# Narrower weights in one of the two products with V: 68 of 128 columns, and V kept as high, low in every head

## The chip, the cores and the metric

The kernel runs on one core of a Trainium2 chip. The metric is the device time of one execution in microseconds (us). The kernel before was timed three times: 2116.72, 2116.77 and 2116.83 us, median 2116.77 us. One further execution was recorded by the hardware profiler; its page and trace are what the text below reads.

The engines have short names in the profile: PE is the matrix engine, PEld its weight loads (which overlap its products), DVE the vector engine, ACT the scalar engine, POOL the engine for general work, SP the one that starts most transfers. Times are us unless marked ns.

## The reference

The model is a decoder trunk of two layers over 1024 positions with 1024 channels. Layer 0 mixes tokens by a gated unit in chunks of 128 positions, layer 1 by a dilated attention; each is followed by a feed-forward block with squared ReLU. The part that matters here is the attention, cut to its core:

```python
def _dilated_group(q, k, v, bias_table, window, dilation):
    ...
    s = jnp.einsum('bnqrhc,bnkrhc->bnrhqk', qb, kc) * (HEAD_DIM ** -0.5)
    ...
    m = jnp.max(logits, axis=-1)
    p = jnp.exp(logits - m[..., None])
    den = jnp.sum(p, axis=-1)
    num = jnp.einsum('bnrhqk,bnkrhc->bnqrhc', p, vc)
```

There are 8 heads of 64 channels and three groups with (window, dilation) = (128, 1), (512, 4) and (2048, 16). Their numerators and denominators are merged for each head, and the quotient goes through an output projection. The last line, the numerator, is the product that the change touches.

## The kernel before

All large products are made with numbers split in two: a high half, rounded to the matrix engine's format, and a low half, what the rounding left. A product of two split numbers is then the sum of high by high, high by low and low by high. Helpers record every such operation: line 197 issues each matrix product, line 204 each transposition through the matrix engine, lines 225 and 226 the two halves of a split (ACT rounds, DVE subtracts).

The attention is worked off in twelve units: four pairs of heads, and for each the three groups. For a unit the queries and keys are computed by seven products of blocks (`unit_qk`, written out in program order). Beside them run three generators for every unit's four steps: `scores` (queries by keys, then bias, minimum and exponential on DVE and ACT), `turned` (the probabilities transposed by the matrix engine and split into a high half `ph` and a low half `pl`), and `values` (the product with V). The order on the matrix engine is fixed while the program is written: a clock that counts each product by the columns of its moving operand (`flow.pe`) says when a generator's next step is due. The count does not look at how many columns the weights have.

V is computed once for all positions before the attention. `value_store` splits it and writes it to DRAM, 64 columns of a half at a time: tile `vs` has shape (128 positions, 4 pairs of heads, 4 quarters, 64). Before the change the quarters of a pair of heads A, B are: A high, A low, B low, B high. `v_load` fetches a pair's 256 columns back into two tiles `V`.

In `values` the two heads of a pair are handled one after the other. For each block of 128 keys the weights are two quarters of V, that is 128 columns with one head's high and low half; they are loaded twice, once for the product with `ph` (e = 0) and once for the product with `pl` (e = 1). A product's moving operand is 128 or 256 columns wide (one or two blocks of queries). All of them add up in one bank `pv`: 64 of its rows hold the sum with V's high half, the other 64 the sum with V's low half. Lines 1551 and 1552 then add the two sets of rows: ACT copies one into `N`, DVE adds the other. Of the four products of halves, low by low is included before the change.

There are 432 products with V in all: for a pair of heads 32 with dilation 4, 32 with dilation 16 and 44 with dilation 1. In the profile they are `at<-tr,V`, and `at<-p,V` in the last unit. Half of them are of the kind e = 1.

Of the kernel before, what the change touches and what calls it, by code (L numbers as in the profile page):

```python
# [19 lines left out]
P = 128  # L20
# [15 lines left out]
def blk(b, n=1):  # L36
    return slice(b * P, (b + n) * P)
# [81 lines left out]
STEPS = (5, 3)  # L119
ROOTS = ((0, 7, 0, 1, 0), (1, 7, 0, 1, 2))  # L120
GATE, ROWS, RB = 6, 10000, 5
ASIDE = {768: (4,)}
EARLY = 4
PACE = (1700.0, 1800.0, 3000.0)
# [4 lines left out]
def trunk(ctx: ExitStack, tc: tile.TileContext, xT, w_u, w_v, w_o, w_s, b_s, w_qkv, w_vt, w_bo, rel,  # L129
# [23 lines left out]
    def slot(shape=(P, S), dtype=F32, name="s"):  # L153

        return slots.tile(list(shape), dtype, tag="s", name=name)
# [37 lines left out]
    def at_bank():  # L193
        return psa.tile([P, HALF], F32, tag="at", name="at")

    def matmul(out, lhsT, rhs, passes=1, **kw):
        nc.tensor.matmul(out, lhsT, rhs, **kw)  # L197
        n = 1
        for d in rhs.shape[1:]:
            n *= d  # L200
        flow.pe(max(n, 64) * COL * passes)
# [26 lines left out]
    def weight(src, own=None):  # L228
        lo = wpool.tile([P, D], F32R, tag="w", name="wlo")
        hi = wpool.tile([P, D], F32R, tag="w", name="whi")  # L230
        for i in range(2):
            split(hi[:, half(i)], lo[:, half(i)], load(src[:, half(i)], own and own()))
        return hi, lo
# [500 lines left out]
    for gi, chunks in enumerate(((0, 1, 2), (3, 4, 5), (6, 7))):  # L734
        banks = {}
        for k in range(KT):
# [7 lines left out]
            with tc.issue_after(roots[0] if k == 1 else gelus[5]) if gi == 1 and k else nullcontext():  # L744
                w = weight(w_v[k])
# [26 lines left out]
            for e, i, n, f in order:  # L772
                x, c = ys[n // 4][k], blk(n % 4)
                matmul(banks[n, f], x[e == 1][:, c], w[e == 2][:, half(f)], start=(k == 0 and e == 0),
                       stop=(k == 7 and e == 2))
# [29 lines left out]
    for tiles in ((0, 1, 2), (3,), (4,), (5, 6, 7)):  # L805
        w = [weight(w_u[m]) for m in tiles]
# [14 lines left out]
    for tiles in ((0, 1), (2,), (3,), (4, 5, 6, 7)):  # L821
        w = [weight(w_o[m]) for m in tiles]
# [359 lines left out]
    hd = [[dram.tile([P, HALF], F32, name=f"hd{m}_{s}", bufs=1) for s in range(2)] for m in range(KT)]  # L1182
# [51 lines left out]
    for hp, g in units:  # L1234
        u = Unit()
# [52 lines left out]
    def value_store(r, b, src):  # L1288
        v = slot((P, 4, 4, 64), F32R, "vs")
        p4 = src.rearrange("p (u a c) -> p u a c", u=4, a=2)  # L1290
        hi, lo = v[:, :, 0:4:3, :], v[:, :, 1:3, :]
        nc.scalar.activation(hi, p4, AF.Copy)
        nc.vector.tensor_tensor(lo, p4, hi.bitcast(F32), op=ALU.subtract)
        nc.sync.dma_start(vd[r][blk(b)], v.bitcast(F32))
# [24 lines left out]
    def all_values():  # L1319

        operands, wv = value_operands(), []
        for s in range(2):
            ks = range(KT) if s == 0 else [4 * j + k for k in range(4) for j in range(2)]
            banks = [mm_bank() if s == 0 and x < 3 else at_bank() for x in range(4)]
            for n, k in enumerate(ks):
                y = terms_a.blocks[k // 4, s]
                flow.until(lambda: len(y) > k % 4)
                for b, bank in enumerate(banks):
                    x, w, c = y[k % 4], firsts[k], blk(b)
                    matmul(bank, x.hi[:, c], w.hi, start=(k == 0), stop=False)  # L1330
                    matmul(bank, x.hi[:, c], w.lo, start=False, stop=False)
                    matmul(bank, x.lo[:, c], w.hi, start=False, stop=(k == KT - 1))
                    flow.pump()
                if s:
                    wv.append(next(operands))
            for b, bank in enumerate(banks):
                value_store(0, 4 * s + b, bank)
# [10 lines left out]
        for n, p in enumerate(VSEQ):  # L1348
# [11 lines left out]
            for b, bank in enumerate(banks):  # L1360
                u, k1 = uk[b][:, 0, :], uk[b][:, 1, :]
                for k in range(4):
                    flow.until(lambda: len(x) > k)
                    c, last = blk(b), k == 3
                    matmul(bank, x[k].hi[:, c], w[k].hi, start=k == 0 and opens, stop=False, skip_group_check=True)
                    matmul(bank, x[k].hi[:, c], w[k].lo, start=False, stop=False, skip_group_check=True)
                    matmul(bank, x[k].lo[:, c], w[k].hi, start=False, stop=last, skip_group_check=True)
                    flow.pump()
                if p in (1, 6):
                    nc.scalar.activation(u, bank, AF.Copy)  # L1370
                elif p == 2:
                    value_store(1, b, added(u, bank))
                elif p == 5:
                    nc.scalar.activation(k1, bank, AF.Copy)
                elif p == 7:
                    value_store(2, 4 + b, added(k1, bank))
                elif p == 3:
                    value_store(1, 4 + b, added(u, bank))
                else:
                    value_store(2, b, bank)  # L1380
                if 0 < n < 6:
                    wv.append(next(operands))
                elif n == 6 and b:
                    more()
# [26 lines left out]
    def place(g, kb):  # L1411

        return (kb % 2, kb // 2) if g == 1 else (kb // 4, kb % 4)
# [66 lines left out]
    def geometry(g, j):  # L1480

        if g == 2:
            keys = [(2 * j, 1), (2 * j + 1, 1)]
        elif g == 1:
            keys = [(2 * j, 1), (2 * j, 2)]
        else:
            keys = [(2 * j - 1, 2) if j else (0, 1), (2 * j, 2)]
        at = [0, keys[0][1] * P]
        return keys, at, at[1] + keys[1][1] * P
# [40 lines left out]
    def values(u, j, pts):  # L1530
        keys, at, _ = geometry(u.g, j)

        parts = {}
        for i in range(2):
            for x in range(keys[i][1]):
                parts.setdefault(keys[i][0] + x, []).append((at[i] + x * P, i * P))
        pv = at_bank()
        for hd in range(2):
            lst = list(parts.items())
            for n, (kb, cs) in enumerate(lst):  # L1540
                pc, oc, w = cs[0][0], hd * 2 * P + cs[0][1], len(cs) * P
                tv, at_ = place(u.g, kb)
                va = u.V[tv][:, at_, 2 * hd:2 * hd + 2, :]
                for e in range(2):
                    matmul(pv[:, oc:oc + w], va, pts[hd][e][:, pc:pc + w], start=(hd == 0 and n == 0 and e == 0),
                           stop=(n == len(lst) - 1 and e == 1), skip_group_check=True)
        for hd in range(2):
            r, x = slice(64 * hd, 64 * hd + 64), slice(64 - 64 * hd, 128 - 64 * hd)
            o, c = u.N[r, 2 * j * P:(2 * j + 2) * P], slice(hd * 2 * P, (hd + 1) * 2 * P)
            with tc.high_priority(offset=PRIO):  # L1550
                nc.scalar.activation(o, pv[x, c], AF.Copy)
                nc.vector.tensor_tensor(o, o, pv[r, c], op=ALU.add)
# [41 lines left out]
    def valuer():  # L1594
        for n, (i, j) in enumerate(seq):
            u = U[i]
            yield turned_at[n], LAT["turn"]
            yield u.v, 0
            if j == 0:
                if u.hp > 0:  # L1600
                    yield rested[u.hp - 1], 0
                u.N = slot(name="N")
            yield from turn_for(CALM[2])
            values(u, j, turned_p.pop(n))
            valued_at[n].t = flow.t
            if j == 3:
                u.pv.t = flow.t
            if u.g == 0 and j % 2:
                valued[u.hp, j // 2].t = flow.t
            yield 0  # L1610
# [242 lines left out]
    def final(sq):  # L1853
# [5 lines left out]
        out = outT.rearrange("(k p) t -> p k t", p=P)  # L1859
        aside = ASIDE.get(sq.cols.start, ())  # L1860
        if aside:
# [89 lines left out]
```

## Time and profile before

| what | value |
|---|---|
| timed, median of three | 2116.77 us |
| the profiled execution, first to last instruction | 2116.2 us |
| granted clock of the matrix engine, mean | 0.998 |
| PE busy | 2093.6 us (99%), 10160 products |
| PEld busy | 1731.2 us (82%), 10160 loads |
| DVE busy, ACT busy | 1577.5 us (75%), 1182.7 us (56%) |
| products with V | from 1085.1 to 1443.7 us of the span |

Some 0.5 us of the timed median lies outside the profiled span. In a row of the profile, `at<-tr,V 128*128 128x256` means: written is a bank `at`, read are the moving operand `tr` and the weights `V`, the array is used with 128 rows by 128 columns, and the moving operand has 256 columns. Products and loads are pipelined: the recorded length of one is longer than the step from one to the next, so a rate is read from several in a row.

### The profile page before, as it was taken

What the parts mean: (1) busy time and instruction counts of PE and PEld (TensorE: products, weight loads), DVE (VectorE), ACT (ScalarE), POOL (GpSimd) and SP (SyncE); (2) the same over time, 40 slices, a digit from 0 to 9 for tenths busy, and PEclk for the clock granted to TensorE, in tenths of its full rate; (3) what the DMA queues carried; (4) which work ended last, traced back from release to release, by engine and by line L of the source; (5) the groups of instructions that cost most, each with busy time, mean ns of one, the idle gap of its engine ahead of it and who ended that gap; (6) DMA issues with size and microseconds to landing.
All of it is one profiled execution on the core that took longest, in us unless ns stands there. A gap on an engine that the chain in (4) does not pass through costs nothing.

```text
span 2116.2 us, 30735 instructions
## 1 busy us (share of the span) xinstructions
PE 2093.6 (99%) x10160; PEld 1731.2 (82%) x10160; DVE 1577.5 (75%) x2902; ACT 1182.7 (56%) x2387; POOL 495.5 (23%) x368
## 2 busy tenths in 40 slices
PE   9999999999999999999999999999999999999998
PEld 7888888888888888788888888888888888888887
DVE  7878769766689999787746666757985456988876
ACT  7645436566675555345456665776556556544432
POOL 2000124323224333430000000002442222433244
PEclk9999999999999999999999999999999999999999
DMA  6428814588766666644865657582266443655432
GB/s 220 130 94 294 305 34 139 196 281 278 258 208 204 231 209 225 222 162 164 308 194 160 176 156 185 157 270 79 71 205 198 156 154 127 203 164 161 143 115 80
DMA packets 224757, 387.10 MB, mean 183 GB/s; under 512 B 39898, under 2 KB 67669, under 8 KB 224597
## 3 DMA queue, kind: packets, MB, share of 16 engines
q1 hardware_dynamic: 215456, 383.77, 55.1%
q10 hardware_dynamic: 9140, 1.36, 0.4%
q8 instruction: 80, 1.31, 0.3%
q14 instruction: 81, 0.66, 0.1%
HBM read 252.24 MB, written 132.81 MB: 182 GB/s over the span
## 4 chain that ended last, share of the span: by engine, by line
PE 88%; DVE 6%; DMA 3%; issue 1%; ACT 1%; POOL 0%; SPq 0%; DVEq 0%; POOLq 0%; ACTq 0%
PE mm L197 45%; PE at L197 41%; PE at L204 2%; DVE y L226 1%; DMA t<-in_w_qkv 1%; DVE t L226 1%; DMA r<-in_w_v 1%; DMA h<-in_xT 0%; DVE r L443 0%; DVE hx L226 0%; DVE tr L226 0%; DVE wp L226 0%; DMA t<-hid_(1, 0)_6229 0%; DMA r<-in_w_vt 0%; DVE b L448 0%
## 5 line engine op out<-in xcount | busy, mean ns | idle before, releaser
L226 DVE TENSOR_TENSOR wp<-r,wp 128x512 fp32r<-128x512 f32 (+3 forms) x399 | 328.2, 828 | 121.8 <-ACT wp L225 119.2
L225 ACT ACTIVATE wp<-r 128x512 fp32r<-128x512 f32 (+3 forms) x399 | 236.0, 596 | 316.7 <-PE at L197 194.5
L197 PE MATMUL mm<-t,wp 128*128 128x512 f32 x1368 | 345.2, 396 | 0.2 <-DVE t L1001 0.2
L197 PE MATMUL at<-hx,wp 128*128 128x512 f32 x1452 | 341.1, 389 | 1.7 <-DVE h L1079 1.5
L197 PEld LDWEIGHTS at<-hx,wp 128*128 128x128 f32 x1452 | 272.2, 188 | 60.0 <-DVE h L1079 3.2
L197 PEld LDWEIGHTS mm<-t,wp 128*128 128x128 f32 x1368 | 250.7, 188 | 53.0 <-issue 0.7
L283 POOL TENSOR_TENSOR t<-t 128x512 f32<-128x512 f32 (+1 forms) x60 | 76.2, 1271 | 810.3 <-ACT t L278 808.1
L197 PE MATMUL at<-y,wp 128*128 128x512 f32 x1008 | 245.3, 389 | 0.0
L197 PE MATMUL mm<-hx,wp 128*128 128x512 f32 x984 | 234.3, 389 | 0.1
L197 PEld LDWEIGHTS at<-y,wp 128*128 128x128 f32 x1008 | 189.1, 188 | 39.5 <-issue 0.4
L197 PEld LDWEIGHTS mm<-hx,wp 128*128 128x128 f32 x984 | 184.6, 188 | 38.9 <-ACT mm L1102 0.5
L197 PE MATMUL mm<-y,wp 128*128 128x512 f32 x816 | 210.3, 397 | 1.2 <-DVE y L226 0.6
L381 POOL TENSOR_TENSOR t<-r 128x512 f32<-128x512 f32 (+3 forms) x62 | 82.5, 1331 | 477.7 <-DMA r<-in_w_up 121.3
L197 PEld LDWEIGHTS mm<-y,wp 128*128 128x128 f32 x816 | 149.1, 188 | 33.4 <-DVE y L226 1.1
L226 DVE TENSOR_TENSOR hx<-t,hx 128x512 fp32r<-128x512 f32 x192 | 161.5, 845 | 6.5 <-ACT hx L225 6.3
L197 PE MATMUL mm<-y,whi 128*128 128x512 f32 x512 | 158.4, 390 | 1.2 <-DVE t L789 1.2
L197 PE MATMUL at<-t,wp 128*128 128x512 f32 x552 | 130.6, 389 | 0.0
L225 ACT ACTIVATE hx<-t 128x512 fp32r<-128x512 f32 x192 | 118.7, 627 | 20.8 <-DMA t<-hid 12.5
L383 POOL TENSOR_TENSOR r<-r 128x512 f32<-128x512 f32 (+3 forms) x62 | 91.0, 1468 | 167.2 <-DVE wp L226 146.9
L197 PEld LDWEIGHTS at<-t,wp 128*128 128x128 f32 x552 | 103.6, 188 | 21.5
L1079 DVE TENSOR_TENSOR h<-h,at 128x512 f32<-128x512 f32 x144 | 97.6, 678 | 25.6 <-PE at L197 25.1
L197 PEld LDWEIGHTS mm<-y,whi 128*128 128x128 f32 x512 | 95.5, 188 | 21.0 <-issue 1.6
(247 smaller groups left out, 3481.3 us busy)
## 6 DMA issues: line engine op xcount, KB each, us to landing
t<-hid SPq DMA_DIRECT2D x182, 256.0 KB, 4.2
wd<-tr SPq DMA_DIRECT2D x154, 256.0 KB, 3.1
wp<-wd SPq DMA_DIRECT2D x77, 512.0 KB, 4.2
hid<-t SPq DMA_DIRECT2D x140, 256.0 KB, 2.9
r<-in_w_up SPq DMA_DIRECT2D x120, 256.0 KB, 2.9
r<-in_w_dn SPq DMA_DIRECT2D x80, 256.0 KB, 2.6
hid<-b SPq DMA_DIRECT2D x56, 256.0 KB, 2.9
r<-in_w_v SPq DMA_DIRECT2D x48, 256.0 KB, 3.1
```

Of the source, the lines that this page charges most:

```text
L197: nc.tensor.matmul(out, lhsT, rhs, **kw)
L204: nc.tensor.transpose(out, src, ident)
L225: return (nc.scalar.activation(hi, src, AF.Copy).ins, (engine or nc.vector).tensor_tensor(lo, src, hi.bitcast(F32), op=ALU.subtract).ins)
L226: (engine or nc.vector).tensor_tensor(lo, src, hi.bitcast(F32), op=ALU.subtract).ins)
L283: nc.gpsimd.tensor_tensor(self.acc, self.acc, sq, op=ALU.add)
L381: tt(r3, r[0, 0], r[1, 0], op=ALU.subtract)
L383: tt(r[1, 1], r[1, 0], r[0, 0], op=ALU.subtract)
L1079: return engine.tensor_tensor(hs[i, s], hs[i, s], src, op=ALU.add).ins
```

## The change

Two things are changed. V's quarters in a pair of heads become A high, A low, B high, B low, so that each head's weights begin with its high half. And in `values`, the product with `pl` takes the first 68 of the 128 weight columns: the 64 of V's high half and four of its low half. It writes 68 rows of the bank. The product with `ph` keeps all 128. Of low by low, only four columns of 64 are still computed; the other 60 are left out of the sum.

```diff
+NARROW = 68
...
     def value_store(r, b, src):
         v = slot((P, 4, 4, 64), F32R, "vs")
         p4 = src.rearrange("p (u a c) -> p u a c", u=4, a=2)
-        hi, lo = v[:, :, 0:4:3, :], v[:, :, 1:3, :]
+        hi, lo = v[:, :, 0:4:2, :], v[:, :, 1:4:2, :]
         nc.scalar.activation(hi, p4, AF.Copy)
         nc.vector.tensor_tensor(lo, p4, hi.bitcast(F32), op=ALU.subtract)
         nc.sync.dma_start(vd[r][blk(b)], v.bitcast(F32))
...
             for n, (kb, cs) in enumerate(lst):
                 pc, oc, w = cs[0][0], hd * 2 * P + cs[0][1], len(cs) * P
                 tv, at_ = place(u.g, kb)
-                va = u.V[tv][:, at_, 2 * hd:2 * hd + 2, :]
-                for e in range(2):
-                    matmul(pv[:, oc:oc + w], va, pts[hd][e][:, pc:pc + w], start=(hd == 0 and n == 0 and e == 0),
-                           stop=(n == len(lst) - 1 and e == 1), skip_group_check=True)
+                va = u.V[tv][:, at_, 2 * hd:2 * hd + 2, :].rearrange("p a c -> p (a c)")
+                for e, m in enumerate((P, NARROW)):
+                    matmul(pv[0:m, oc:oc + w], va[:, 0:m], pts[hd][e][:, pc:pc + w],
+                           start=(hd == 0 and n == 0 and e == 0), stop=(n == len(lst) - 1 and e == 1),
+                           skip_group_check=True)
```

No instruction changes its place on any engine, and none is added or removed. On the matrix engine the 216 products with e = 1 have 68 weight columns in place of 128. Here is the end of one group of eight with its neighbours, on PE in the first unit, before (`tr` are the split probabilities, `wp` the weights of queries and keys):

```order
1448 L197 MATMUL at<-tr,V 128x128 x2
1449 L197 MATMUL at<-tr,V 128x256 x2
1450 L197 MATMUL at<-tr,V 128x128 x2
1451 L197 MATMUL mm<-t_9778,wp 128x512 x3
1452 L204 MATMUL at<-ident,t 128x128 x6
```

and the same place with the change:

```order
1449 L198 MATMUL at<-tr,V 128x128
1450 L198 MATMUL at<-tr,V 68x128
1451 L198 MATMUL at<-tr,V 128x256
1452 L198 MATMUL at<-tr,V 68x256
1453 L198 MATMUL at<-tr,V 128x128
1454 L198 MATMUL at<-tr,V 68x128
1455 L198 MATMUL mm<-t_9778,wp 128x512 x3
1456 L205 MATMUL at<-ident,t 128x128 x6
```

A wide and a narrow product now alternate; what stands ahead of them and behind them is the same. Every line number after the new constant is one or more higher.

## The prediction, on record before the changed kernel was run

> **What bounds the kernel now.** I read the page first, from the busy shares to the chain that ended last:
>
> ```profile
> PE 2093.6 (99%) x10160; PEld 1731.2 (82%) x10160; DVE 1577.5 (75%) x2902; ACT 1182.7 (56%) x2387; POOL 495.5 (23%) x368
> ...
> PEclk9999999999999999999999999999999999999999
> ...
> PE 88%; DVE 6%; DMA 3%; issue 1%; ACT 1%; POOL 0%; SPq 0%; DVEq 0%; POOLq 0%; ACTq 0%
> ```
>
> The matrix engine is never long without work, and the chain is 88% its own. The change touches only the stretch with products by V, so I read that stretch (the attention) in the view of busy times, and the chain inside it:
>
> ```profile
> 1085.00:1447.00 362.00, 360.06 (x2295) 298.23 (x2294) 237.11 (x784) 242.73 (x689) 0.00 (x0) 1.00 0.59 176
> ...
> by line: PE mm L197 64.4%; PE at L197 24.0%; PE at L204 10.3%; DVE t L1688 0.8%; DVE tr L226 0.6%; issue 0.0%
> ```
>
> The columns are PE, PEld, DVE, ACT and POOL busy, then the granted clock (1.00), the share of the transfer engines and GB/s. DVE and ACT have a third of the 362 us free, the transfer engines 41%. The chain is the matrix engine's for 98.7%. So here time taken from PE comes off the end, unless PE runs into another engine that it now outruns.
>
> A busy PE can still be limited by its weight loads. The groups of the products with V, each shape by itself:
>
> ```profile
> L197 PEld LDWEIGHTS at<-tr,V 128*128 128x128 f32 x388 | 50.7, 190 | 4.3 <-DVE tr L226 0.9
> L197 PE MATMUL at<-tr,V 128*128 128x128 f32 x276 | 40.3, 260 | 0.0
> L197 PE MATMUL at<-tr,V 128*128 128x256 f32 x112 | 25.3, 304 | 0.0
> L197 PEld LDWEIGHTS at<-p,V 128*128 128x128 f32 x44 | 5.6, 190 | 0.3
> L197 PE MATMUL at<-p,V 128*128 128x128 f32 x28 | 4.4, 255 | 0.0
> L197 PE MATMUL at<-p,V 128*128 128x256 f32 x16 | 3.6, 303 | 0.0
> ```
>
> There are 276 + 28 = 304 products that stream 128 columns and 112 + 16 = 128 that stream 256. Their rate is seen in one group of eight with 128 columns, in the timeline of PEld from the group's second load on, and in the busy times of the V products in the same stretch:
>
> ```profile
> 1120.65 0.86 PEld L197 LDWEIGHTS at<-tr,V 128*128 128x128 f32 x7
> ...
> 1120.64:1121.42 0.78, 0.78 (x8) 0.77 (x7) 1.00 0.24 83
> ```
>
> Seven loads take 0.86 us from the first start to the last end. With 190 ns for the last one, six steps take 0.67 us: **112 ns a step**. PEld is busy for 0.77 of 0.78 us, so it has a load under way all the time. What would the streams need alone? The shortest recorded product with 128 columns has 220 ns, one with 512 columns 389 ns:
>
> ```profile
> L197 PE MATMUL at<-tr,V x388: 220/275/387, 1085.4 to 1430.3; 128*128 128x128 f32 x138, 128*128 128x256 f32 x56
> ...
> L197 PE MATMUL at<-y,wp 128*128 128x512 f32 x1008 | 245.3, 389 | 0.0
> ...
> 1119.28 1.52 PE L197 MATMUL mm<-y,wp 128*128 128x512 f32 x6
> ```
>
> The 384 columns between them cost 169 ns, 0.44 ns each; the last row gives the same rate, (1.52 - 0.389) / 5 = 0.226 us for 512. So 128 columns stream in 56 ns and 256 in 113 ns. Where a product has 128 columns, the next load (112 ns) sets the step, and half of the step the array has nothing to stream. Where it has 256, stream and load are equal.
>
> **The change, part by part.**
>
> *The narrow load.* A load runs under the product ahead of it: that of e = 1 under the product e = 0 of the same block and the same width. So 304 / 2 = 152 narrow loads stand behind a product of 128 columns and 128 / 2 = 64 behind one of 256. The trace has no load of 68 columns. It has six of 8 columns, as a summary of tile `tab` and in the timeline of PEld:
>
> ```profile
> L197 PEld LDWEIGHTS at<-tr,tab x6: 82/84/86, 447.6 to 488.4; 33*8 33x8 f32 x6
> ...
> 447.59 0.09 PEld L197 LDWEIGHTS at<-tr,tab 33*8 33x8 f32 x2 [0.35 <-issue]
> 448.03 0.30 PEld L197 LDWEIGHTS mm<-t,wp 128*128 128x128 f32 x2 [0.35 <-issue]
> ```
>
> A load of 8 columns has 84 ns, one of 128 has 190: 106 ns for 120 columns, 0.88 ns each. The starts agree: two loads of 8 columns take 0.09 us together, so the second began within 0.01 us of the first, where two of 128 in the row below take 0.30 us and began 0.11 us apart. The whole 0.11 us is therefore column time, and not a fixed cost of a load. Rows do not explain it: the loads `at<-k,q` in the same list have 64 rows and 186 ns:
>
> ```profile
> L197 PEld LDWEIGHTS at<-k,q 64*128 64x128 f32 x576 | 36.7, 186 | 17.5 <-issue 7.5 <-DVE tr L226 3.0 <-DVE t L1688 2.3
> ```
>
> 60 columns fewer are then 60 x 0.88 = 53 ns less, and the step falls from 112 to 59 ns. The stream of 56 ns lies just below, so it takes nothing back. I take 52 ns: **152 x 0.052 = 7.9 us less**. Bounds: 0 if a load takes its time whatever its width; 152 x (112 - 56) = 8.5 us if the stream alone sets the step. I stay near the upper one, because 8 and 128 columns lie on one line through nearly zero. For the price of 68 columns itself the Trainium skill, "TensorE: Matmul & The Clock Gate", section LDWEIGHTS, has a rule: columns divided by 1.2 ns, which is 57 ns; with that the step would be 57 and the sum 152 x 0.055 = 8.4 us.
>
> *The 64 narrow loads behind 256 columns* save nothing: the stream's 113 ns cover the load of 112 now and would go on covering one of 59. The 216 loads of e = 0 are unchanged, too; each still needs 112 ns, and where it stands behind a narrow product of 128 columns it sets the step. So a pair of products goes from 224 to 171 ns, not to 118. A group of eight with 128 columns should lose four times 52 ns, 0.21 us; one with widths 256, 256, 128, 128 twice over, two times, 0.10 us.
>
> *What the faster groups run into.* PE saves at most 0.21 us in one group; is what it asks for next already there? The waits of PEld in the attention, and the idle time before the loads of V in the summary of that tile:
>
> ```profile
> PEld at L197 <- issue: 6.8, 22, 0.4
> PEld at L197 <- DVE tr L226: 3.5, 13, 0.4
> PEld at L197 <- DVE t L1688: 2.3, 3, 0.8
> PEld at L197 <- ACT tr L225: 2.2, 6, 0.4
> ...
>   DVE tr L226: 0.9, 4
> ...
> 1088.77 1.02 DVE L226 TENSOR_TENSOR tr<-at,tr 128x384 fp32r<-128x384 f32 x2
> ...
> 1091.24 0.87 PEld L197 LDWEIGHTS at<-tr,V 128*128 128x128 f32 x6
> ```
>
> Only four times in 48 groups does a load of V wait for the split probabilities, 0.9 us in all. The last two rows are the ordinary case: the split ends at 1089.79, the group begins at 1091.24, 1.45 us of slack against a gain of 0.1. The other rows with `tr` lie before `at<-k,q` (3.0 us of them, by its row above) and have the length of those named "issue", 6.8 / 22 = 0.31 us: it is the price of going to products with 64 rows, and stays. Left are some ten true waits (these four, three for line 1688, a few for N). Such a wait grows by what PE saved since its cause, about 0.1 us: **1.0 us back**. Bounds: 0, and 33 waits (all but "issue") by 0.21 us, 6.9 us.
>
> *V's new order.* 24 tiles are split with both halves in runs of 64. For ACT this is so before; for DVE the low half was in runs of 128. The rows of ACT and DVE for such tiles:
>
> ```profile
> L1293 DVE TENSOR_TENSOR vs<-t,vs 128x512 fp32r<-128x512 f32 x12 | 8.2, 687 | 2.0 <-ACT vs L1292 1.7
> L226 DVE TENSOR_TENSOR tr<-N,tr 128x512 fp32r<-128x512 f32 x6 | 4.2, 694 | 1.4 <-PE at L197 1.4
> ```
>
> A low half that is written in one run costs 694 ns, one in runs of 128 costs 687; runs of 64 should cost the same to 10 ns, at most 24 x 0.01 = 0.2 us of DVE time either way, under PE's own work before the attention. The transfers keep their number, sizes and places. The two operations that empty `pv` read what they read before. All this I cost at 0.
>
> *Sum.* 7.9 - 1.0 = 6.9 us off the profiled 2116.2 us, 2109.3 us of span; the median of the runs, 2116.77, lies 0.5 us above the span, so **2109.9 us**. What comes behind the attention is released by PE or by buffers that it empties, and shifts as a whole.
>
> **The rivals.**
>
> *No shorter load.* The array might be filled by 128 shifts whenever a product uses it whole; the loads of 8 columns belong to products that use only a part of it. Then nothing changes: 2116.8 us. For it: no load of 9 to 127 columns was recorded. Against it: load time that follows the columns as above. The Trainium skill, "TensorE: Matmul & The Clock Gate", section on weight-path modes, would add a reason to be slower: a fast load exists only for 128 columns and not for 32-bit floats, so a narrow one would lose it. But here the split weights load at 190 ns and the unsplit 32-bit ones no slower, so I see no fast load to lose:
>
> ```profile
> L197 PEld LDWEIGHTS at<-ones,t 128*128 128x128 f32 x136 | 17.2, 191 | 2.2 <-DVE t L287 0.9 <-POOL t L283 0.5
> ```
>
> If columns counted in strips of 32, 68 would load as 96: 32 x 0.88 = 28 ns less, 152 x 0.028 = 4.3 us, with 0.6 us given back 2113.1 us. The step of at most 10 ns at 8 columns speaks against strips.
>
> *The gain is eaten by waits.* The list has 33 waits for other engines; if most of them are true and grow by 0.16 us (between 0.10 and 0.21), 5.3 of the 7.9 us go and 2114.2 us are left. Against it: the slack above.
>
> *Slower: the narrow product drains the array.* At the loads of `tab` PEld stood idle for 0.35 us going in and 0.35 us coming out: the array empties when the part of it in use changes. Were 68 columns such another part, each of 216 pairs would pay this twice. Its price: from the first of these rows of PE to the third are four products of 512 columns and two of 384,
>
> ```profile
> 446.59 1.07 PE L197 MATMUL mm<-t,wp 128*128 128x512 f32 x4
> 447.59 0.52 PE L197 MATMUL at<-tr,tab 33*8 33x384 f32 x2
> 448.04 0.50 PE L197 MATMUL mm<-t,wp 128*128 128x512 f32 x1
> ```
>
> which stream in 4 x 0.226 + 2 x 0.169 = 1.24 of the 1.45 us. 0.21 us for two changes, and 0.11 us for the load that is then exposed, is 0.16 us a change; 432 changes cost 69 us, less the 7.9 us: 2178 us. It decides as soon as a change costs more than 7.9 / 432 = 18 ns. Against it: all 128 rows stay in use, and 68 columns need the array past its half. The Trainium skill, "TensorEngine Tiling", sections Available Configurations and Key Properties, says that changing the tiling drains the array and knows columns of 128, 64 and 32 only; 68 would then be plain 128, and this rival would fall.
>
> **How the numbers follow.** The forecast has 0.77, "no shorter load" 0.09, strips of 32 columns 0.03, gain eaten by waits 0.08, draining 0.03. What a measurement of this kernel can tell from no change is about 0.2%, 4.2 us, so faster means below 2112.5 and slower above 2121.0 us. The forecast's own bounds, with 8.5 us and nothing given back, and with 7.4 us and 2.5 given back, are 2108.3 to 2111.9, all faster. A fifth of the case of eaten gains falls there too: faster 0.79. The rest of that case, strips and no shorter load: same 0.18. Slower: 0.03. The range goes up to 2113.6, past the strips and the mild half of the eaten gains, and leaves out some 0.17.
>
> **What would show it.** In the profile after, PEld's rows for V split into 216 loads of 128 columns at 190 ns and 216 of 68 near 137 ns, and a group of eight with 128 columns ends 0.2 us sooner. Steps of 112 ns throughout would show the loads unshortened; idle time named "issue" before V's loads, the drain; the same groups shorter but PEld's waits for `tr` and N several us longer, the eaten gain. I am wrong if the attention's stretch shrinks by less than 4.5 us, or if what it gains is lost behind 1447 us.

## The result and the profile after

The changed kernel takes 2112.24 us (median of 6 runs, 2108.62 to 2114.67) where the kernel before, run beside it, takes 2116.80 us. The ratio is 0.9972, with a 95% interval of 0.9961 to 0.9984: 5.9 us less, between 3.4 and 8.3 (the two medians are 4.6 us apart; the ratio takes in all runs). Forecast were 2109.9 us, 6.9 us less.

The profiled execution has a span of 2112.9 us. First the same parts of its page as before (busy shares, granted clock, chain):

```profile
PE 2086.2 (99%) x10160; PEld 1724.8 (82%) x10160; DVE 1578.7 (75%) x2902; ACT 1183.1 (56%) x2387; POOL 496.5 (23%) x368
...
PEclk9999999999999999999999999999999999999999
...
PE 83%; DVE 8%; DMA 4%; ACT 2%; issue 1%; POOL 1%; SPq 0%; DVEq 0%; POOLq 0%; ACTq 0%
```

PE's busy time is 7.4 us shorter, that of DVE and ACT the same to 1.2 us. The chain has lost 5 points of PE to the others. Next the groups of loads with V, by shape, and the timeline of PEld for the group of eight of which the prediction showed seven loads:

```profile
L198 PEld LDWEIGHTS at<-tr,V 128*128 128x128 f32 x194 | 35.8, 189 | 1.7
L198 PEld LDWEIGHTS at<-tr,V 128*68 128x68 f32 x194 | 27.2, 140 | 3.9 <-DVE tr L227 2.3
L198 PEld LDWEIGHTS at<-p,V 128*128 128x128 f32 x22 | 4.1, 190 | 0.2
L198 PEld LDWEIGHTS at<-p,V 128*68 128x68 f32 x22 | 3.1, 140 | 0.2
...
1122.79 0.89 PEld L198 LDWEIGHTS at<-tr,V 128*128 128x128 f32 x8
1123.60 0.77 PEld L198 LDWEIGHTS mm<-t,wp 128*128 128x128 f32 x4
```

The same two lines in the kernel before are:

```profile
1120.42 1.08 PEld L197 LDWEIGHTS at<-tr,V 128*128 128x128 f32 x8
1121.42 0.54 PEld L197 LDWEIGHTS mm<-t,wp 128*128 128x128 f32 x3
```

A narrow load has 140 ns instead of 190, and the eight loads take 0.89 us instead of 1.08. From the group's first load to the first behind it: 0.81 us, before 1.00. Four of its eight steps have become 0.05 us shorter.

For the whole attention I take the stretch from the first load of V to the start of the last product with V, in the view of busy times, of the kernel before and after:

```profile
1085.10:1443.70 358.60, 356.66 (x2275) 295.27 (x2273) 235.45 (x781) 240.78 (x686) 0.00 (x0) 1.00 0.59 175
```

```profile
1088.10:1440.60 352.50, 349.08 (x2275) 287.57 (x2274) 234.93 (x780) 239.95 (x685) 0.00 (x0) 1.00 0.60 178
```

It is **6.1 us** shorter. Yet the spans differ by 3.3 us only: after, the attention began 3.0 us later, at 1088.1 instead of 1085.1. Of this, 1.7 us come from two waits near 900 us, in a stage that the change does not touch. The waits of PEld in the window 880 to 925 us, before and after:

```profile
PEld mm L197 <- ACT mm L1102: 1.4, 2, 0.9
```

```profile
PEld mm L198 <- ACT mm L1103: 3.1, 2, 1.7
```

Behind the attention both take the same, 672.5 and 672.3 us (span less the end of the stretch).

### The profile page after: what moved, and what is told of

It reads as the page before. It is cut to its first block, busy times and chain, and to the rows that moved or that the text cites. A ratio compares the mean times of both kernels' runs of the same rounds, so it can differ in the third digit from the quotient of the medians.

```text
span 2112.9 us, 30735 instructions
## 1 busy us (share of the span) xinstructions
PE 2086.2 (99%) x10160; PEld 1724.8 (82%) x10160; DVE 1578.7 (75%) x2902; ACT 1183.1 (56%) x2387; POOL 496.5 (23%) x368
## 4 chain that ended last, share of the span: by engine, by line
PE 83%; DVE 8%; DMA 4%; ACT 2%; issue 1%; POOL 1%; SPq 0%; DVEq 0%; POOLq 0%; ACTq 0%
PE mm L198 42%; PE at L198 40%; PE at L205 2%; DMA t<-in_w_qkv 1%; DVE tr L227 1%; DVE y L227 1%; DVE q L1438 1%; DMA h<-in_xT 1%; DMA r<-in_w_vt 0%; DVE hx L227 0%; DMA t<-hid_(0, 0)_6227 0%; DMA r<-in_w_v 0%; DVE wp L227 0%; DMA ex<-sc 0%; ACT tr L226 0%
```

## The experiments

In all of them the theory, called load theory in the expectations, is the prediction's: a step in a chain of products costs the longer of the running product's stream and the next product's load, so a narrow load gains only where a product of 128 columns runs ahead of it. The rivals were named ahead of each run.

### The new order of V by itself

```diff
-NARROW = 68
+NARROW = 128
```

> Only V's new order is kept; both products load all 128 columns. If the gain comes from the narrow loads, nothing is left of it: every load of V at 190 ns, a group of eight with 128 columns again at 1.116 us from its first load to the start of the load after the next product (as before the change), PE busy about 2093 us as before, median within 2 us of the kernel before. If the new order itself helped (or hurt) the split or the transfers, some of the 6 us gained in the attention (from the first load of V to the last product with V) would stay, and the attention would be shorter than 358.6 us.

Measured: 2117.06 us, ratio to the kernel before 1.0002 (0.9993 to 1.0012). The attention takes 358.4 us, and DVE's groups for V's split are as before. Its view of busy times, and V's split on DVE:

```profile
1084.30:1442.70 358.40, 356.48 (x2275) 295.25 (x2273) 235.52 (x781) 240.83 (x686) 0.00 (x0) 1.00 0.59 175
...
L1294 DVE TENSOR_TENSOR vs<-t,vs 128x512 fp32r<-128x512 f32 x12 | 8.3, 688 | 2.0 <-ACT vs L1293 1.7
```

688 ns for runs of 64, 687 before for runs of 128. The order gives and costs nothing that shows: of the 6.1 us in the attention 0.2 are there, so the gain comes with the narrow product.

### Narrow only where 256 columns stream

```diff
-                for e, m in enumerate((P, NARROW)):
+                for e, m in enumerate((P, NARROW if len(cs) == 2 else P)):
```

> 68 columns only in the 64 products with e = 1 that stream 256 columns, where a product of 256 columns covers the load; the 152 others load 128 again. Load theory (a load costs only what the stream ahead of it does not cover): no gain, each group as long as before, median within 2 us of the kernel before, although 64 loads record 140 instead of 190 ns. Rival (the product itself is cheaper with 68 rows written, not its load): 64 of 216 products keep their gain, about 50 ns each, so 3.2 us in PE's busy time and 0.10 us off each group with widths 256, 256, 128, 128.

Measured: 2116.92 us, ratio 1.0001 (0.9992 to 1.0010). The narrow loads are there, and the attention hardly differs:

```profile
L198 PEld LDWEIGHTS at<-tr,V 128*68 128x68 f32 x56 | 7.9, 141 | 1.1 <-DVE tr L227 0.2
...
1083.90:1441.90 358.00, 356.02 (x2274) 295.00 (x2273) 235.38 (x781) 240.61 (x686) 0.00 (x0) 1.00 0.60 175
```

64 loads are 50 ns shorter each, 3.2 us in all, but PE's busy time is only 0.4 us shorter (2093.2 us) and 0.6 us of the attention is gone. Of this 0.5 us lies in six groups that wait for the split probabilities; one of them is 0.23 us shorter, and with the new order alone it differs by 0.11 us already. Among the others, by the starts of their loads, a group with widths 256, 256, 128, 128 is 3 to 11 ns shorter, not 100. So a narrow product is not cheaper in itself: the time was in loads that the product ahead did not cover.

### 64 columns instead of 68

```diff
-NARROW = 68
+NARROW = 64
```

> 64 columns instead of 68 in the product with the low half: all four columns of V's low half are gone from it too. If load time only follows the columns: 137 ns a load instead of 140, and a group of eight with 128 columns at 0.91 us as with 68 (the stream of 56 ns already sets the step), time within 2 us of the kernel after. If 64 columns put the array into another tiling, which drains it on the way in and out as at the loads of 8 columns: 432 changes at 0.1 to 0.16 us, 43 to 69 us more, and idle time named issue ahead of V's loads: about 2160 to 2178 us.

Measured: one execution at 2112.27 us, attention 352.7 us. The loads of one group with 128 columns:

```profile
1119.95 0.88 PEld L198 LDWEIGHTS at<-tr,V 128*128 128x128 f32 x8
1120.75 1.23 PEld L198 LDWEIGHTS mm<-t,wp 128*128 128x128 f32 x6
```

0.80 us from first load to first load behind, where 68 columns have 0.81 (unrounded 803 and 805 ns), and a mean load of 136 ns (`at<-tr,V 128*64`, against 140). There is no drain with 64 columns, and so no sign that the slower rival of the prediction holds at 68. That the four columns beyond 64 cost time does not show in one execution.

### The same products in another order

```diff
+            wide = [x for x in parts.items() if len(x[1]) == 2]
+            rest = [x for x in parts.items() if len(x[1]) == 1]
+            lst = [(x, e) for x in rest for e in range(2)]
+            if wide:
+                lst = [(wide[0], 0)] + lst + [(wide[0], 1)]
+            for n, ((kb, cs), e) in enumerate(lst):
...
+                m = NARROW if e else P
```

With it a head's products run: 256 columns by wide weights, 128 by wide, 128 by narrow (twice these two with dilation 1), 256 by narrow.

> Where a head has a block of 256 query columns, its wide-weight product stays first and its narrow-weight product goes last, so that 64 loads of 128 columns that now stand behind a narrow product of 128 columns stand behind a product of 256. Load theory: each of these steps falls from 112 to 59 ns, 64 x 0.053 = 3.4 us less PE time than the kernel after (mixed groups of eight 0.10 us shorter than there, of twelve 0.10 us), about 2109 us, ratio to the kernel before 0.9955. Rival (a product with 68 rows is cheaper wherever it stands): the same products, the same time as the kernel after, 2112 us.

Measured: 2108.44 us, ratio 0.9959 (0.9947 to 0.9972). The loads of the first group, here and in the kernel after:

```profile
1083.05 0.92 PEld L198 LDWEIGHTS at<-tr,V 128*128 128x128 f32 x8
1083.89 0.55 PEld L198 LDWEIGHTS mm<-t,wp 128*128 128x128 f32 x3
```

```profile
1088.06 1.01 PEld L198 LDWEIGHTS at<-tr,V 128*128 128x128 f32 x8
1088.99 0.54 PEld L198 LDWEIGHTS mm<-t,wp 128*128 128x128 f32 x3
```

0.84 instead of 0.93 us from first load to first load behind: 0.09 of the expected 0.10 us. The products are the same, only what runs ahead of each load is not; a product that was cheaper in itself would have given nothing here. By the starts of the loads, the groups without 256 columns are as long as in the kernel after (to 2 ns), those with them mostly 0.055 to 0.10 us shorter, 2.5 us together. (This is taken to the second load behind each group: here a group ends with 256 columns, which the first load behind still runs under, so that counting to it would show 3.0 us.) The attention takes 350.4 us, 2.1 less than in the kernel after, where 3.4 were expected.

```profile
1083.10:1433.50 350.40, 346.79 (x2275) 285.21 (x2274) 234.38 (x780) 238.91 (x685) 0.00 (x0) 1.00 0.60 179
```

The expectation took 0.10 us for each mixed group, and that was too much by a quarter; another 0.4 us is lost between the groups; at which places was not followed up.

### The changed kernel once more

The kernel is the changed one, unaltered.

> The changed kernel once more, unaltered, beside the runs below. Its runs so far spread over 6 us (2108.6 to 2114.7) and those of the kernel before over 5 us, and in the profile the changed kernel was 2.8 us behind the one before where the first load of V stands, ahead of anything that the change touches. If that is chance of single executions, this profile stands elsewhere at that point, and the ratio over more runs is that of the 6.1 us counted from there to the end: 2110.7 us, ratio 0.9971. If the new order of V cost something ahead of the attention, it stands behind again, by about 3 us.

Measured: 2110.22 us (5 runs), ratio 0.9968 (0.9955 to 0.9980). The first load of V stands at 1086.3 us, not at 1088.1, and the attention takes 352.8 us:

```profile
1086.30:1439.10 352.80, 349.19 (x2274) 287.33 (x2273) 234.84 (x780) 240.02 (x685) 0.00 (x0) 1.00 0.59 178
```

In the kernels of this study that place lay at 1083.1 to 1088.1 us, although all of them do the same up to V's split at 950 us; the kernel with the new order alone had it at 1084.3, earlier than the kernel before. So the new order of V does not cost the 3.0 us ahead of the attention; they differ from one execution to the next. In both sets the profiled execution of the changed kernel was the slowest (2114.67 us of six, 2113.15 of five). Why that place moves is open. The gain inside the attention returned to 0.3 us.

### The six groups that wait, put off

Six groups of products with V wait for the split probabilities in the kernel after (more on them below). This puts off the third step of seven units, the six groups among them:

```diff
-            yield turned_at[n], LAT["turn"]
+            yield turned_at[n], LAT["turn"] + (1400.0 if j == 2 and u.g < 2 and i < NU - 1 else 0.0)
```

> The changed kernel, with the third group of values in a unit of dilation 1 or 4 (not in the last unit) put off by 1.4 us of the writing clock, that is behind two more blocks of products of 512 columns; the six groups that waited for the split probabilities are among these. If these waits ate what the narrow loads saved there (1.2 us) and what they cost before (1.2 us), the idle time before loads of V named after the split falls from 3.3 us to under 1 us, and the attention is 1.5 to 2.5 us shorter than in the kernel after. If the split is late because ACT and DVE are behind with other work, the wait moves to another product (scores or transpositions that come later too) and nothing is gained.

Measured: 2123.79 us, ratio 1.0029 (1.0019 to 1.0038), slower than before. No load of V waits for the split any more, but in the attention PEld now waits for something else:

```profile
PEld mm L198 <- DVE k L1438: 12.5, 7, 2.2
PEld at L198 <- issue: 7.0, 24, 0.4
PEld at L198 <- ACT N L1553: 3.9, 10, 0.7
```

In the kernel after, the first of these rows does not occur. Line 1438 makes the low half of the keys, on DVE, and PE's next products wait until it is done; the attention takes 363.6 us. The second outcome that the expectation named, at a higher price: the wait moved, and grew. That these waits can be had back by a better place is neither shown nor excluded.

### 64 columns in the new order of products

> The order of e4_regroup with 64 columns instead of 68. A narrow load is then 3 ns shorter and just under the stream of 56 ns; about 10 ns off a mixed group and 5 ns off one with 128 columns were seen between 68 and 64 columns, 48 groups, 0.4 us: the time of e4_regroup less 0.4 us, 2108 us, ratio to the kernel before 0.996.

Measured: 2108.39 us, ratio 0.9955 (0.9943 to 0.9968), attention 350.2 us. As expected it is not to be told from 68 columns in that order. It is the fastest kernel of the study by a hair; the kernel after, run beside it, had 0.9968, and the intervals overlap. That the order of products helps rests on the attention, 350.4 and 350.2 us against 352.5 and 352.8.

### Each product by itself between products of 512 columns

```diff
+                    if apart and (hd == 0 or n < len(lst) - 1 or e == 0):
+                        yield 1
...
+            apart = i < NU - 1
             yield from turn_for(CALM[2])
-            values(u, j, turned_p.pop(n))
+            if apart:
+                calm[0] += HOLD
+            yield from values(u, j, turned_p.pop(n), apart)
```

`HOLD` is 3000 ns.

> The products of values are no longer in one block: each stands by itself between three products of 512 columns (not in the last unit). Load theory: behind every product of 128 columns, wide or narrow, now comes a load of 128 columns, so each takes 112 ns again, and the narrow loads stand behind 512 columns, where they save nothing. The attention is back near the 358 us of the kernel before, and near 2116 us in all, although the same 68 columns are loaded. Rival (a product with 68 rows is cheaper wherever it stands): the 6 us stay, about 2111 us. Other waits can shift either of these by some us; the steps of the loads decide.

Measured: one execution at 2174.57 us, far from both numbers: the attention takes 424.9 us, with 17.9 us of PE waiting for the transfers of V and 15.6 us of PEld for line 1513 (the minimum of the scores, on DVE), and a granted clock of 0.93. Probably the late values hold buffers that the next fetch of V needs; this was not followed up. The total decides nothing. The steps do, where nothing waits and the granted clock is 1.00; the timeline of PEld, in a stretch where every product with V streams 128 columns:

```profile
1129.13 0.19 PEld L199 LDWEIGHTS at<-tr,V 128*128 128x128 f32 x1
1129.36 0.53 PEld L199 LDWEIGHTS mm<-t,wp 128*128 128x128 f32 x3
1129.93 0.14 PEld L199 LDWEIGHTS at<-tr,V 128*68 128x68 f32 x1
1130.16 0.53 PEld L199 LDWEIGHTS mm<-t,wp 128*128 128x128 f32 x3
1130.74 0.19 PEld L199 LDWEIGHTS at<-tr,V 128*128 128x128 f32 x1
1130.97 0.54 PEld L199 LDWEIGHTS mm<-y,wp 128*128 128x128 f32 x3
1131.56 0.14 PEld L199 LDWEIGHTS at<-tr,V 128*68 128x68 f32 x1
```

Wide to narrow 0.80 and 0.82 us, narrow to wide 0.81: the same for both. A narrow load behind a product of 512 columns gains nothing. Less the three others (3 x 0.226 = 0.68), each product with V costs 0.13 us, near the load behind it of 112 ns and more than twice its own stream of 56.

## Why the prediction was right, point by point

**PE's time is the end's time in the attention:** yes. The attention is 6.1 us shorter (5.8 in the repetition), and nothing of it is lost behind 1447 us.

**The narrow load.** Columns set the price: 140 ns measured, 137 forecast by the line through 8 and 128 columns. The step was to fall from 112 to 59 or 60 ns (52 ns saved). By the starts of the loads in the kernel after, where nothing waits (medians), the step from a load behind 128 columns to the next load is 111 ns for 128 columns and 61 for 68; behind 256 columns it is 118 and 120. Group by group, from the starts of the loads in both traces, a group with four narrow loads behind 128 columns is 0.20 us shorter and one with two 0.10, 50 ns a load. 152 x 0.050 = 7.6 us, forecast 7.9; PE's busy time says 7.4.

**The 64 loads behind 256 columns save nothing:** shown by the kernel that has only these (ratio 1.0001, and 3 to 11 ns a group).

**What the faster groups run into.** Forecast 1.0 us back. Of 48 groups, 42 are shorter by the full amount, 6.8 us together. The other six wait for the split probabilities, and are 0.35 us longer in all instead of 0.9 us shorter: 1.25 us back. Between the groups 0.4 us more is lost; at which places was not followed up. That is 1.7 us, well over the term and far from its bound of 6.9. One of the six, the loads of PEld and the splits on DVE before and after:

```profile
1157.71 0.19 PEld L197 LDWEIGHTS at<-tr,V 128*128 128x128 f32 x1
1158.18 1.33 PEld L197 LDWEIGHTS at<-tr,V 128*128 128x128 f32 x11 [0.28 <-DVE tr L226]
...
1157.43 1.29 DVE L226 TENSOR_TENSOR tr<-at,tr 128x512 fp32r<-128x512 f32 x2
```

```profile
1159.13 0.19 PEld L198 LDWEIGHTS at<-tr,V 128*128 128x128 f32 x1
1159.93 1.15 PEld L198 LDWEIGHTS at<-tr,V 128*68 128x68 f32 x11 [0.62 <-DVE tr L227]
...
1159.19 1.29 DVE L227 TENSOR_TENSOR tr<-at,tr 128x512 fp32r<-128x512 f32 x2
```

The second load needs the low half of the probabilities. Counted from the first load of V, the group begins 1.49 us earlier than before, the split only 1.15 us: the wait went from 0.28 to 0.62 us, and the group kept nothing. The difference is about what PE saved in the two groups just ahead (0.10 and 0.20 us). The prediction had counted four waiting loads with 0.9 us in all from the summary of tile V; after, the same row has eight with 3.3 us, but it counts products too: five are loads, with 2.3 us, and three are products that wait for the same splits:

```profile
  DVE tr L227: 3.3, 8
```

The mechanism is the one that the prediction named, a wait that grows by what PE saved since its cause; the size is not. Some ten waits were to grow by 0.1 us each. Instead six grew, by 0.08 to 0.50 us, and cost 0.2 us a group. In the case shown the cause lies further back than one group. Counted from the first load of V, the work of DVE and ACT had been 1.16 us early (to within 0.02 us) since about 1141 us of the kernel before; in the last 12 us ahead of the split, each longer wait that their timelines name is of one of these two engines for the other, and what PE saved there did not bring them forward. The other five groups were not taken apart in this way, and putting the groups off made it worse.

**The new order of V at 0:** shown by the kernel with it alone (1.0002, to 0.1%).

**The time.** 2109.9 us were forecast, 2112.24 and 2110.22 us measured in two sets of runs; the difference of the two sets is nearly as large as the larger miss. Both lie in the stated range, but the first lies 0.3 us above the forecast's own bounds (2108.3 to 2111.9). In the attention 6.0 us came off (unrounded) where 6.9 were forecast: the gain was 7.7 us (6.8 in 42 groups and the 0.9 that the six would have had) and not 7.9, and 1.7 were given back and not 1.0, so no two errors cancel. One step of the sum is misread: the 0.5 us between the median and the profiled span set one execution beside others. In each run of the record the time lies 1.7 to 1.8 us above that same run's span, so by this estimate the profiled execution before took some 1.2 us more than the median. The forecast does not hang on it, as it comes to the median less 6.9 us. The profiled span was forecast as 2109.3 us and came as 2112.9 and 2111.4, with 3.0 and 1.2 us of that lost ahead of the attention.

**The rivals.** A load that takes its time whatever its width, and strips of 32 columns (96 columns would be 162 ns by the same line), fall by the 140 ns. The drain falls with the group that is 0.19 us shorter, where it would have been longer, and with 64 columns there is none either. The eaten gain is there in six groups of 48, at 1.25 us (1.7 with what is lost between the groups), not at 5.3.

## What to carry to other kernels

In a chain, a product with few moving columns can cost as much as the load of the next one (here 112 ns). So count, for every load, the columns that stream ahead of it: here a narrower load paid where that stream is shorter than the load (128 columns, 56 against 112 ns), and neither behind 256 columns nor behind 512. Once some loads are narrow, put the long streams ahead of the full ones: here that gave 2.1 us more in the attention, with the same products. Where all loads are alike, as in the kernel before, this count gives an order of products nothing to win; that was not run. Before a gain per group is multiplied by the groups, look for those that already wait for another engine: here most of the six that kept nothing or little had waited before.

## What the runs showed of the hardware that was not expected

Weights of 64 columns between weights of 128 cost nothing extra: behind products of 128 columns, the step from the start of a load to the start of the next (medians) is 61 ns for a load of 64 columns and 109 ns for one of 128, side by side and without idle time at the changes, where going to the products with 64 rows leaves PEld idle for 0.3 us each time (6.8 us in 22 waits). And one execution differs from the next by up to 5 us ahead of 1085 us, although the program there is the same: the place of V's first load is 1083.1 to 1088.1 us in the ten profiles, all of kernels with the same program up to there but for V's order. Both kernels' times spread by as much, so 0.2% is close to what single executions can tell, and the stretch of the trace that the change touches tells far more.
